# Two transformer blocks on one core: a fifth plain product block in each FFN, and five smaller edits around it

## The chip, the cores and the metric

The kernel runs on one core of a Trainium2 chip. The metric is the time of one execution on the device, in microseconds (us). Engines are named as in the profile: PE is TensorE (matmuls), DVE is VectorE, ACT is ScalarE, POOL is GpSimd, SP is the queue that issues the transfers of the weights.

## What is computed

Two transformer blocks follow each other, with 512 positions, a width of 1024 and float32 values. The first block has a mixer of two attentions and one FFN; the second an FFN, a mixer of sparse attention and retention, another FFN and a last norm. The three FFNs have the same form, and most of the change lies in them:

```python
def _swiglu(x, w_gate, w_up, w_down):
    return (jax.nn.silu(x @ w_gate) * (x @ w_up)) @ w_down

h = h + swiglu(rms_norm(h, norm_ffn_g), w_ffn_gate, w_ffn_up, w_ffn_down)      # f0, in the first block
...
h = h + 0.5 * _swiglu(_rmsnorm(h, ...), ...)                                   # f1 and f2, in the second
```

The hidden width is 2816. In the second mixer, the keys and values of the sparse attention are compressed by small networks (`gelu(blk @ w1) @ w2`), whose weights w1 come into the text below. The norm of the second mixer's input has gains of its own.

## The kernel before, in words

**Precision.** Each float32 operand is held as a high and a low part, and each product is three matmuls: high by high, high by low, low by high. The high part of a weight is a cast on ACT (`wh`, L235 and L300), the low part a subtraction on DVE (`wl`, L236 and L303) or, for some, on POOL. The operand x has `xh` (an ACT cast, L363) and `xl` (a DVE subtraction, L370).

**An FFN** (`ffn`, L1324). The 2816 hidden columns are 22 blocks of 128, in two halves of 11. After each half the down product of that half is added to the residual `xs`. In the first half the first `NPLAIN` blocks, here 4, are plain products: g and u each take 8 x 3 matmuls of 128x512, into one bank each of the two "mm" banks. All other blocks are units (`unit`, L1225): a product scheme that needs seven quarter products in place of eight, each 12 matmuls of 128x256, in the order B11, T1, T4 of the unit before, T2, B21, B22, T3. T4 of a unit is held back (`pending`) and run by `flush()` in the next unit, or behind the last one. A unit's weight sums (s13, s24) are made by DVE in PSUM tiles with the tag "ss", two tiles of two banks each.

**The entry of an FFN.** The first plain block is computed on x without its norm, since the norm's factor is not known yet. It is summed over the columns and spread to all partitions by two matmuls with a diagonal matrix (`spread`, L440, `diag` by DVE L437), and ACT copies the result to `rb` (L442). Each plain block then takes, in this order, fg = g x rb (DVE L1356), tanh (ACT L1357), fu = u x rb (DVE L1358), u x fg (POOL L1359), ft (DVE L1360), and the high and low parts hh and hl of the result. Behind each of the four blocks `prepare_t` makes a quarter of the operand for the units' T products, th and tl, out of the normed rows y (L1204) and their differences ts; `prepare_b`, behind the last plain block, rewrites xh and xl as the parts of y, for the units' B products. The unit's first product, B11, reads these xh and xl; its result is copied by ACT into tile "fu" (L1251), the same tile that holds u of the plain blocks (one buffer), and T2 is added in the same bank after that copy.

**What sets the order.** A scheduler orders each engine's instructions from the program's text and its own estimates. `in_order` pins the units of a first half in the order of the text, and in a second half only the units from number NPLAIN on, so the first NPLAIN units of a second half are left to the scheduler. Weights come by the SP queue, two blocks ahead.

**The second mixer** (`second_mixer`, L1401). It computes keys, values and gates by tokens (L584 to L586) on x without its norm; ACT scales the result by the norm's factor into `kvg` (L1408). Among these products the norm's factor is spread as in an FFN. `renorm` then multiplies xs by gain and rb (DVE L469) and casts xh (ACT) and xl (DVE) anew for the products that follow. The weights w1 of the compression come by POOL's own transfers (L1601), two tiles at a time, with a cast on ACT and a subtraction on POOL (L370); their products are L1607 and L1608.

**The end** (`last`, L1961). The second down product of f2 is computed by tokens, two groups t of 256 rows, with L1982 for its products and with the transposed residual (`turn_out`, L1954) in between. The result is added to the residual (L2009), squared and summed, normed and stored. It begins with a flush of the last unit's T4 and a new set of PSUM banks:

```python
self.flush()()
self.psum("ps4")
```

Of the kernel before, what the change touches and what calls it, by code (L numbers as in the profile page):

```python
# [10 lines left out]
F32 = mybir.dt.float32  # L11
# [8 lines left out]
P = 128  # L20
# [9 lines left out]
RAW_BUFS, PART_BUFS, AHEAD = 4, 5, 2  # L30
NPLAIN = 4
KEEP = 2
# [301 lines left out]
class Build:  # L334
# [989 lines left out]
    def ffn(self, tag, scale, gain, hooks, on_out, begun=None, each=None, last=None):  # L1324
        nc, att = self.nc, self.att
        n = 0
        self.th, self.tl, self.ynorm = [], [], {}
        for half in range(2):
            hh, hl = [], []
            for i in range(11):  # L1330
                if half or i >= NPLAIN:
                    if i in (0, NPLAIN):
                        start = len(self.traced())
                    self.unit(f"{tag}{half}{i}", hh, hl, i)
                    if i == 10:
                        self.in_order(start)
                    continue
                acc = []
                for w in "gu":
                    wh, wl = self.ws.next(f"{tag}{w}{half}{i}")  # L1340
                    self.ws.run_ahead()
                    b = self.bank("mm")
                    self.drain(self.tgroup(b, [(wh[:, k, :], wl[:, k, :], self.xh[k], self.xl[k]) for k in range(KD)]))
                    acc.append(b)
                    if n < len(hooks):
                        hooks[n]()
                    n += 1
                    if n == 2 * NPLAIN - 1:
                        u = self.first_unit(f"{tag}0{NPLAIN}")
                        u.hi24()  # L1350
                        u.lo24()
                if i == 0 and begun is not None:
                    begun()
                tl = lambda t, bufs=1: att.tile([P, 512], F32, tag=t, name=self.nm(t), bufs=bufs)
                g, th, u = tl("fg"), tl("ft", 2), tl("fu")
                nc.vector.tensor_tensor(out=g, in0=acc[0], in1=self.rb, op=ALU.mult)  # L1356
# [4 lines left out]
                self.put_hidden(i, th, 0.5, hh, hl)  # L1361
                self.prepare_t(i, gain)
                if i == NPLAIN - 1:
                    self.prepare_b()
            if half == 1 and last is not None:
                last(hh, hl)
                return
            for m in range(KD):
# [14 lines left out]
                if half == 0 and each is not None:  # L1383
                    each(half, m)
                if scale == 1.0:
# [7 lines left out]
    def second_mixer(self, acc, qpool, eq):  # L1393
# [21 lines left out]
        for m in range(KD):  # L1415
            self.renorm(m, self.xs[m], self.gain("mix_norm_2", m))

        turned = [0]
# [154 lines left out]
    def nsa_keys(self, kvg, need, N):  # L1573
# [17 lines left out]
        for kind in "kv":  # L1591
# [7 lines left out]
            for q in range(4):  # L1599
                w1 = kp.tile([P, 4, 256], F32, tag="w1", name=self.nm("w1"), bufs=2)  # L1600
                nc.gpsimd.dma_start(out=w1, in_=w1v[:, 4 * q:4 * q + 4, :])  # L1601
                wh, wl = (kp.tile([P, 4, 256], F32R, tag=f"w1{a}", name=self.nm("w1"), bufs=2) for a in "hl")
                self.hi(wh, w1)
                self.lo(wl, w1, wh, eng=nc.gpsimd)
# [259 lines left out]
    def main(self):  # L1864
# [53 lines left out]
        def each(half, m):  # L1918
            x = self.xs[m]
            nc.vector.scalar_tensor_tensor(out=x, in0=x, scalar=gf(m), in1=N["rbf"], op0=ALU.mult, op1=ALU.mult)  # L1920
# [40 lines left out]
        def last(hh, hl):  # L1961

            self.flush()()
            self.psum("ps4")
            mm = nc.tensor.matmul
# [3 lines left out]
            for t in range(2):  # L1969

                cut = [((0, 256), (256, 512)) if (t, i, f) == (1, 1, 1) else ((0, 512),) for i in range(2) for f in range(2)]
                tags = self.TOKTAGS[t] + ("mm",)
                acc = [[self.bank(tags[q + n]) for n in range(len(c))] for q, c in enumerate(cut)]
                held = []
# [10 lines left out]
                for k in range(11):  # L1985
# [5 lines left out]
                    for q in range(4):  # L1991
                        for n in range(len(cut[q])):
                            products(w, k, q, n)
                    if t == 0 and k == 0:
                        nc.gpsimd.dma_start(out=gb, in_=I["final_norm_2"][None, :].to_broadcast([P, D]))
                    if t == 0:
# [48 lines left out]
```

## Time and profile before

| | us |
|---|---|
| median of three runs | 2081.18 |
| lowest and highest | 2079.14, 2083.57 |
| the profiled execution | 2081.28 |
| its span, first to last instruction | 2079.4 |
| PE busy in it | 2021.3 (97%) |
| DVE busy | 1479.1 (71%) |
| ACT busy | 1047.5 (50%) |
| POOL busy | 557.3 (27%) |

The profiled execution takes 1.9 us more than its span, for what lies around the first and the last instruction. PE is busy nearly everywhere, so its waits are few and can be counted one by one. The busy shares of the other engines say little: they are means over a long program, and an engine with a share of 71% can be the last to finish in one stretch. In the views below, a bracket behind a row is the time that the engine stood idle before it, and what ended that.

### The profile page before, as it was taken

To read this page: it belongs to the slowest core of one execution; us is meant where nothing else is said; L and a number is where in the kernel's file an instruction comes from. 1 tells how busy PE (TensorE), PEld (TensorE's weight loads), DVE (VectorE), ACT (ScalarE), POOL (GpSimd) and SP (SyncE) were. 2 spreads that over 40 slices of the span, in tenths; PEclk is the share of its full clock that TensorE was granted. 3 is DMA by queue.
4 is the path that set the end of the run, shared out by engine and by line. 5 is a ranking of instruction groups with operands and counts; after the bars stand their busy time and mean duration, and the time that the engine had idled before them with its cause. 6 is when DMAs were issued, how large, how long until landed. Compare 5 with 4: busy or idle time off the path is not lost. (4 is left out here: it accounts for less than half of the span.)

```text
span 2079.4 us, 31555 instructions
## 1 busy us (share of the span) xinstructions
PE 2021.3 (97%) x11802; PEld 1750.8 (84%) x11802; DVE 1479.1 (71%) x2745; ACT 1047.5 (50%) x1959; POOL 557.3 (27%) x469
## 2 busy tenths in 40 slices
PE   9999999999999999999998999999999999999998
PEld 7787878789899879899986778888888887989987
DVE  7678775776587588568648799888457658746865
ACT  7666753354355435345434576666343333534554
POOL 2233232331132334123234211110412232412310
PEclk9999999999999999999999999999999999999999
DMA  7323254123234313333465322222633441333343
GB/s 204 78 73 84 92 169 130 63 79 113 93 107 121 117 51 97 107 101 106 123 169 141 94 61 78 77 70 68 184 118 105 134 139 51 100 112 99 105 158 128
DMA packets 229528, 223.62 MB, mean 108 GB/s; under 512 B 16784, under 2 KB 190992, under 8 KB 229376
## 3 DMA queue, kind: packets, MB, share of 16 engines
q1 hardware_dynamic: 222992, 203.94, 32.6%
q0 software_dynamic: 5024, 15.90, 2.5%
q8 instruction: 93, 1.52, 0.3%
q10 hardware_dynamic: 1360, 1.77, 0.3%
q14 instruction: 59, 0.48, 0.1%
HBM read 204.11 MB, written 14.68 MB: 105 GB/s over the span
## 5 line engine op out<-in xcount | busy, mean ns | idle before, releaser
L236 DVE TENSOR_TENSOR wl<-raw,wh 128x1024 fp32r<-128x1024 f32 (+5 forms) x261 | 311.2, 1195 | 165.9 <-ACT wh L235 164.5
L235 ACT CAST wh<-raw 128x1024 fp32r<-128x1024 f32 (+5 forms) x261 | 245.9, 945 | 358.1 <-PE mm L397 285.5
L396 PE MATMUL mm<-xh,wh 128*128 128x512 f32 x888 | 364.7, 411 | 11.5 <-ACT kvg L1408 5.1
L397 PE MATMUL mm<-xl,wh 128*128 128x512 f32 x888 | 351.6, 396 | 0.6 <-DVE xl L370 0.5
L398 PE MATMUL mm<-xh,wl 128*128 128x512 f32 x888 | 351.4, 396 | 0.0
L303 POOL TENSOR_TENSOR wl<-raw,wh 128x512 fp32r<-128x512 f32 x108 | 140.9, 1325 | 292.5 <-PE mm L1195 177.1
L396 PEld LDWEIGHTS mm<-xh,wh 128*128 128x128 f32 x888 | 168.5, 190 | 40.9 <-DVE fg L1356 5.9
L398 PEld LDWEIGHTS mm<-xh,wl 128*128 128x128 f32 x888 | 167.6, 189 | 35.7
L397 PEld LDWEIGHTS mm<-xl,wh 128*128 128x128 f32 x888 | 168.6, 190 | 26.9 <-DVE xl L370 2.1
L398 PE MATMUL mm<-hh,wl 128*128 128x512 f32 x440 | 173.4, 394 | 0.0
L397 PE MATMUL mm<-hl,wh 128*128 128x512 f32 x440 | 172.5, 392 | 0.0
L396 PE MATMUL mm<-hh,wh 128*128 128x512 f32 x440 | 170.8, 388 | 0.0
L1195 PE MATMUL mm<-th,wh 128*128 128x256 f32 x432 | 121.1, 280 | 12.2 <-ACT fu L1251 12.2
L303 POOL TENSOR_TENSOR wld<-raw,whd 128x512 fp32r<-128x512 f32 x54 | 74.8, 1386 | 213.1 <-DVE s13f L284 129.1
L613 ACT ACTIVATE P<-s,st 128x128 f32<-128x128 f32 (+1 forms) x192 | 101.4, 529 | 58.4 <-DVE st L608 54.3
L1195 PE MATMUL mm<-th,wl 128*128 128x256 f32 x432 | 120.7, 279 | 0.0
L1195 PE MATMUL mm<-tl,wh 128*128 128x256 f32 x432 | 120.7, 279 | 0.0
L1195 PE MATMUL pt<-xh,wh 128*128 128x256 f32 x432 | 120.2, 278 | 0.0
L1195 PE MATMUL pt<-xl,wh 128*128 128x256 f32 x432 | 120.0, 278 | 0.0
L1195 PE MATMUL pt<-xh,wl 128*128 128x256 f32 x432 | 119.8, 277 | 0.0
L363 ACT CAST ph<-pt 128x128 fp32r<-128x128 f32 x192 | 80.3, 424 | 54.4 <-PE pt L631 53.3
L451 POOL TENSOR_TENSOR sacc<-sacc,sq 128x512 f32<-128x512 f32 x36 | 57.2, 1589 | 165.3 <-ACT sq L449 162.6
(481 smaller groups left out, 5490.1 us busy)
## 6 DMA issues: line engine op xcount, KB each, us to landing
raw<-in_gu_f SPq DMA_DIRECT2D x132, 512.0 KB
raw<-in_w_in SPq DMA_DIRECT2D x79, 512.0 KB
raw<-in_ffn_w_down SPq DMA_DIRECT2D x22, 512.0 KB
raw<-in_ffn_w_down SPq DMA_DIRECT2D x24, 384.0 KB
sp_th<-gt SPq DMA_DIRECT2D x32, 256.0 KB
raw<-in_w_out SPq DMA_DIRECT2D x16, 512.0 KB
raw<-in_ffn_w_down SPq DMA_DIRECT2D x24, 320.0 KB
raw<-in_w_ffn_down SPq DMA_DIRECT2D x16, 384.0 KB
```

The costliest lines, as they stand in the source:

```text
L235: nc.scalar.copy(p[0][:, :nk * nc_], src)
L236: nc.vector.tensor_tensor(out=p[1][:, :nk * nc_], in0=src, in1=p[0][:, :nk * nc_].bitcast(F32), op=ALU.subtract)
L303: (eng or self.ws.b.nc.vector).tensor_tensor(out=p[1], in0=src, in1=p[0].bitcast(F32), op=ALU.subtract)
L363: self.nc.scalar.copy(out, in_)
L396: mm(acc, lhsT=lh, rhs=rh, start=start, stop=False)
L397: mm(acc, lhsT=lh, rhs=rl, start=False, stop=False)
L398: mm(acc, lhsT=ll, rhs=rh, start=False, stop=stop)
L451: (eng or nc.gpsimd).tensor_tensor(out=acc, in0=acc, in1=dst, op=ALU.add)
L613: nc.scalar.activation(p, b, AF.Exp, bias=st[:, 0:1], scale=-1.0, accum_out=st[:, 1:2])
L1195: self.nc.tensor.matmul(acc, lhsT=l[:, sl], rhs=r, start=start and k + n == 0, stop=k == 3 and n == 2, skip_group_check=True)
```

## The change

1. `NPLAIN` goes from 4 to 5: each first half has five plain blocks and six units instead of four and seven. In each second half five units instead of four are left to the scheduler.
2. u of a plain block has a tile of its own ("sq" of the small pool) in place of the units' "fu".
3. Block 1 accumulates g and u in one "ss" tile of two banks (`early`) instead of the two "mm" banks.
4. `prepare_b` stands ahead of the last plain block's elementwise work in the text, and `prepare_t` is called for the first four blocks alone.
5. The residual's scaling that f1 issues in its first down product (`each`) is ordered behind the last DVE instruction of the first half's units.
6. The ACT casts of w1 in the second mixer are ordered behind the last cast of `renorm`.
7. `last` no longer begins with the flush and the new banks. The first group's accumulators are two "ss" tiles, the second group's the "mm" and "pt" banks and half of a third "ss" tile; the flush, with T4 of the last unit, follows the first 12 products.

```diff
@@ -28,7 +28,7 @@
 NEG = -1e30
 MAGIC = 12582912.0
 RAW_BUFS, PART_BUFS, AHEAD = 4, 5, 2
-NPLAIN = 4
+NPLAIN = 5
 KEEP = 2
 
 
@@ -1334,12 +1334,19 @@
                     self.unit(f"{tag}{half}{i}", hh, hl, i)
                     if i == 10:
                         self.in_order(start)
+                        self.last_step = [x for x in self.traced() if x.engine == mybir.EngineType.DVE][-1]
                     continue
                 acc = []
                 for w in "gu":
                     wh, wl = self.ws.next(f"{tag}{w}{half}{i}")
                     self.ws.run_ahead()
-                    b = self.bank("mm")
+                    if i == 1:
+
+                        if w == "g":
+                            early = self.ps.tile([P, 1024], F32, tag="ss", name=self.nm("early"), bufs=2)
+                        b = early[:, 512 * (w == "u"):512 * (w == "u") + 512]
+                    else:
+                        b = self.bank("mm")
                     self.drain(self.tgroup(b, [(wh[:, k, :], wl[:, k, :], self.xh[k], self.xl[k]) for k in range(KD)]))
                     acc.append(b)
                     if n < len(hooks):
@@ -1351,17 +1358,18 @@
                         u.lo24()
                 if i == 0 and begun is not None:
                     begun()
+                if i == NPLAIN - 1:
+                    self.prepare_b()
                 tl = lambda t, bufs=1: att.tile([P, 512], F32, tag=t, name=self.nm(t), bufs=bufs)
-                g, th, u = tl("fg"), tl("ft", 2), tl("fu")
+                g, th, u = tl("fg"), tl("ft", 2), self.small.tile([P, 512], F32, tag="sq", name=self.nm("u"), bufs=1)
                 nc.vector.tensor_tensor(out=g, in0=acc[0], in1=self.rb, op=ALU.mult)
                 nc.scalar.activation(th, g, AF.Tanh, scale=0.5)
                 nc.vector.tensor_tensor(out=u, in0=acc[1], in1=self.rb, op=ALU.mult)
                 nc.gpsimd.tensor_tensor(out=u, in0=u, in1=g, op=ALU.mult)
                 nc.vector.scalar_tensor_tensor(out=th, in0=th, scalar=1.0, in1=u, op0=ALU.add, op1=ALU.mult)
                 self.put_hidden(i, th, 0.5, hh, hl)
-                self.prepare_t(i, gain)
-                if i == NPLAIN - 1:
-                    self.prepare_b()
+                if i < 4:
+                    self.prepare_t(i, gain)
             if half == 1 and last is not None:
                 last(hh, hl)
                 return
@@ -1381,7 +1389,8 @@
                         u.lo24()
                 x = self.xs[m]
                 if half == 0 and each is not None:
-                    each(half, m)
+                    with self.tc.issue_after(self.last_step):
+                        each(half, m)
                 if scale == 1.0:
                     nc.vector.tensor_tensor(out=x, in0=b, in1=x, op=ALU.add)
                 else:
@@ -1414,6 +1423,7 @@
                 self.rb = self.spread(self.r_tok, "rb")
         for m in range(KD):
             self.renorm(m, self.xs[m], self.gain("mix_norm_2", m))
+        self.normed = [x for x in self.traced() if x.engine == mybir.EngineType.Activation][-1]
 
         turned = [0]
 
@@ -1600,7 +1610,8 @@
                 w1 = kp.tile([P, 4, 256], F32, tag="w1", name=self.nm("w1"), bufs=2)
                 nc.gpsimd.dma_start(out=w1, in_=w1v[:, 4 * q:4 * q + 4, :])
                 wh, wl = (kp.tile([P, 4, 256], F32R, tag=f"w1{a}", name=self.nm("w1"), bufs=2) for a in "hl")
-                self.hi(wh, w1)
+                with self.tc.issue_after(self.normed):
+                    self.hi(wh, w1)
                 self.lo(wl, w1, wh, eng=nc.gpsimd)
                 for j in range(4):
                     k = 4 * q + j
@@ -1960,8 +1971,6 @@
 
         def last(hh, hl):
 
-            self.flush()()
-            self.psum("ps4")
             mm = nc.tensor.matmul
             ov = self.out[0].rearrange("(t p) d -> t p d", p=P)
             turned = turn_out()
@@ -1969,8 +1978,12 @@
             for t in range(2):
 
                 cut = [((0, 256), (256, 512)) if (t, i, f) == (1, 1, 1) else ((0, 512),) for i in range(2) for f in range(2)]
-                tags = self.TOKTAGS[t] + ("mm",)
-                acc = [[self.bank(tags[q + n]) for n in range(len(c))] for q, c in enumerate(cut)]
+                two = lambda: self.ps.tile([P, 1024], F32, tag="ss", name=self.nm("two"), bufs=2)
+                if t == 0:
+                    acc = [[b[:, f * 512:(f + 1) * 512]] for b in (two(), two()) for f in range(2)]
+                else:
+                    acc = [[self.bank(a)] for a in ("mm", "mm", "pt", "pt")]
+                    acc[3].append(two()[:, 0:512])
                 held = []
 
                 def products(w, k, q, n):
@@ -1992,6 +2005,7 @@
                         for n in range(len(cut[q])):
                             products(w, k, q, n)
                     if t == 0 and k == 0:
+                        self.flush()()
                         nc.gpsimd.dma_start(out=gb, in_=I["final_norm_2"][None, :].to_broadcast([P, D]))
                     if t == 0:
                         next(turned, None)
```

On PE in f1, at the end of the first plain block: the last matmul of block 0, the four spread matmuls (two broadcasts, `pt`), and block 1. Before:

```order
L398 MATMUL mm_7562<-xh_7103,wl_7472 128x512
L440 MATMUL pt_7587<-diag_7592,ones_r 128x512 x2
L440 MATMUL pt_7599<-diag_7604,ones_r 128x512 x2
L396 MATMUL mm_7644<-xh_7096,wh_7502 128x512
L397 MATMUL mm_7644<-xl_7104,wh_7502 128x512
L398 MATMUL mm_7644<-xh_7096,wl_7503 128x512
```

The same place now:

```order
L398 MATMUL mm_7504<-xh_7045,wl_7414 128x512
L440 MATMUL pt_7529<-diag_7534,ones_r 128x512 x2
L396 MATMUL early_7586<-xh_7038,wh_7444 128x512
L397 MATMUL early_7586<-xl_7046,wh_7444 128x512
L398 MATMUL early_7586<-xh_7038,wl_7445 128x512
L396 MATMUL early_7586<-xh_7039,wh_7444 128x512
L440 MATMUL pt_7541<-diag_7546,ones_r 128x512
L397 MATMUL early_7586<-xl_7047,wh_7444 128x512
L398 MATMUL early_7586<-xh_7039,wl_7445 128x512
L440 MATMUL pt_7541<-diag_7546,ones_r 128x512
```

Block 1 goes to the tile `early`, and the second broadcast stands among its matmuls instead of ahead of them.

On ACT at the first unit of f0: xh are prepare_b's casts, hh the last plain block's result, fu the unit's copy of B11 (L1251). Before:

```order
L363 CAST xh_3638<-y_4108 128x512
L363 CAST xh_3639<-y_4197 128x512
L363 CAST xh_3640<-y_4295 128x512
L365 ACTIVATE hh_4289<-ft_4282 128x512
L1251 COPY fu_4326<-mm_4324 128x256
L1256 COPY ff_4327<-pt_4325 128x256
```

Now:

```order
L363 CAST xh_3638<-y_4107 128x512
L363 CAST xh_3639<-y_4196 128x512
L363 CAST xh_3640<-y_4285 128x512
L1251 COPY fu_4399<-mm_4397 128x256
L365 ACTIVATE hh_4393<-ft_4386 128x512
L1256 COPY ff_4400<-pt_4398 128x256
```

The copy now stands ahead of hh, which needs the last plain block's ft, and directly behind the xh casts.

On ACT at the start of the second mixer: w are the casts of w1, rb the copy of the spread factor, wh weight casts, xh the casts of renorm, kvg the scaled keys and values. Before:

```order
L235 CAST wh_11298<-raw_11131 128x1024
L363 CAST w_1153_11388<-w_1152_11386 128x1024
L363 CAST w_1156_11420<-w_1155_11418 128x1024
L442 COPY rb_11227<-s_11217 128x512
L235 CAST wh_11329<-raw_11161 128x1024
L363 CAST xh_10710<-xs_3584 128x512
L363 CAST xh_10711<-xs_3585 128x512
L1408 ACTIVATE kvg<-mm_11123,rs_11185 128x304
L1408 ACTIVATE kvg<-mm_11124,rs_11185 128x304
```

Now, with the place to which the w1 casts have gone:

```order
L235 CAST wh_11122<-raw_10965 128x1024
L235 CAST wh_11182<-raw_11015 128x1024
L442 COPY rb_11111<-s_11101 128x512
L235 CAST wh_11213<-raw_11045 128x1024
L363 CAST xh_10594<-xs_3584 128x512
L363 CAST xh_10595<-xs_3585 128x512
L363 CAST xh_10596<-xs_3586 128x512
L1417 ACTIVATE kvg<-mm_11007,rs_11069 128x304
...
L363 CAST xh_10600<-xs_3590 128x512
L363 CAST xh_10601<-xs_3591 128x512
L363 CAST w_1147_11272<-w_1146_11270 128x1024
L363 CAST w_1150_11304<-w_1149_11302 128x1024
```

The two casts of w1 have moved from ahead of rb to behind the last xh; one more xh stands ahead of kvg.

## Rows read from the trace of the kernel before

**Rows 1.** PE's waits: line, what it waited for, us in total, times, longest.

```profile
PE mm L1195 <- ACT fu L1251: 12.2, 3, 4.5
PE mm L396 <- ACT kvg L1408: 5.1, 1, 5.1
PE mm L396 <- DVE fg L1356: 4.6, 2, 2.3
...
PE mm L1195 <- DVE xl L370: 3.2, 6, 0.8
PE mm L1195 <- DVE fw L1285: 2.5, 2, 2.0
...
PE mm L396 <- DVE fu L1358: 1.6, 2, 1.0
...
PE pt L440 <- DVE diag L437: 1.2, 1, 1.2
```

**Rows 2.** Windows: span, busy us (count) by engine, granted clock, DMA share, GB/s.

```profile
388.00:391.00 3.00, 2.92 (x7) 2.34 (x8) 1.83 (x4) 0.63 (x1) 2.30 (x2) 0.50 0.51 175
1727.40:1731.00 3.60, 3.60 (x16) 2.93 (x17) 2.41 (x4) 0.57 (x2) 2.43 (x2) 1.00 0.43 150
2005.80:2009.00 3.20, 3.20 (x10) 2.52 (x10) 2.59 (x5) 0.63 (x1) 0.00 (x0) 0.50 0.82 268
```

**Rows 3.** Timeline of PE in a plain block: start us, duration, instruction, [idle before].

```profile
395.80 0.39 PE L396 MATMUL mm<-xh,wh 128*128 128x512 f32 x1
...
397.17 0.39 PE L396 MATMUL mm<-xh,wh 128*128 128x512 f32 x1
```

**Rows 4.** Timeline of PE, the first matmul of f0's block 1.

```profile
388.08 0.79 PE L396 MATMUL mm<-xh,wh 128*128 128x512 f32 x1 [2.29 <-DVE fg L1356]
```

**Rows 5.** Timelines of DVE, then of all engines, at f0's first unit.

```profile
423.42 1.09 DVE L370 TENSOR_TENSOR xl<-y,xh 128x256 fp32r<-128x256 f32 x3
...
427.16 0.68 DVE L1358 TENSOR_TENSOR fu<-mm,rb 128x512 f32<-128x512 f32 x1
...
429.60 0.69 DVE L1360 SCALAR_TENSOR_TENSOR ft<-ft,fu 128x512 f32<-128x512 f32 x1 [1.16 <-POOL fu L1359]
...
430.86 0.35 ACT L1251 COPY fu<-mm 128x256 f32<-128x256 f32 x1
```

**Rows 6.** Groups of DVE, 387.3 to 423.5: count | busy us, mean ns | idle before.

```profile
L1356 DVE TENSOR_TENSOR fg<-mm,rb 128x512 f32<-128x512 f32 x4 | 2.7, 679 | 0.0
L1360 DVE SCALAR_TENSOR_TENSOR ft<-ft,fu 128x512 f32<-128x512 f32 x3 | 2.6, 859 | 1.5 <-POOL fu L1359 1.5
L236 DVE TENSOR_TENSOR wl<-raw,wh 128x1024 fp32r<-128x1024 f32 x2 | 2.4, 1222 | 2.4 <-ACT wh L235 2.4
```

**Rows 7.** Line L370 in f0 (ns, min/median/max), and POOL's timeline there.

```profile
L370 DVE TENSOR_TENSOR tl<-ts,th x8: 674/679/1780, 395.8 to 422.8; 128x512 fp32r<-128x512 f32 x8
...
402.46 1.67 POOL L1359 TENSOR_TENSOR fu<-fu,fg 128x512 f32<-128x512 f32 x1 [2.90 <-DVE fu L1358]
```

**Rows 8.** Timelines of ACT, DVE and POOL at the second mixer's start.

```profile
1091.40 1.05 ACT L363 CAST w<-w 128x1024 fp32r<-128x1024 f32 x1 [1.18 <-DMA w<-in_cmp_k_w]
1092.36 0.57 ACT L442 COPY rb<-s 128x512 f32<-128x512 f32 x1
...
1092.96 4.42 DVE L469 SCALAR_TENSOR_TENSOR xs<-xs,gains,rb 128x512 f32<-128x512 f32 x3 [4.28 <-ACT rb L442]
...
1093.81 2.35 POOL L370 TENSOR_TENSOR w<-w,w 128x1024 fp32r<-128x1024 f32 x1
...
1097.28 1.32 ACT L1408 ACTIVATE kvg<-mm,rs 128x304 f32<-128x304 f32 x3
```

**Rows 9.** Line L1601, the transfers of w1 by POOL: issue to landing.

```profile
DMA to landing us min/median/max: 4.1/4.4/5.5
```

**Rows 10.** Timeline of PE at the end of f2's last unit: T3's last, T4's first.

```profile
2002.03 0.28 PE L1195 MATMUL mm<-th,wl 128*128 128x256 f32 x1
2004.35 0.36 PE L1195 MATMUL mm<-th,whd 128*128 128x256 f32 x1 [2.04 <-DVE fw L1285]
```

## The prediction

> **What bounds the kernel now.** I read the list of TensorE's waits first [rows 1]. It is the right place to start because matmuls fill nearly the whole span, so that a change can win only where TensorE stands still, where its clock is low, or where matmuls go away. Each row names what TensorE waited for, the total, the number of waits and the longest. Six of the seven rows lie in four places that the edits touch. Three are the entries of the three FFNs (f0 near 380 us, f1 near 735, f2 near 1720): from the end of the first plain block to the first units. There stand the wait for the first product's elementwise work (fg L1356, two of 2.3 us), for a bank (fu L1358), for the norm's broadcast (diag, f1 alone), for the low parts of the rewritten operand (xl L370, six) and, largest, for the first unit's copy into "fu" (L1251, three of about 4 us). The fourth place is the start of the second mixer, one wait of 5.1 us for kvg. A last one is the final unit's T4, 2.0 of the fw row.
>
> Then I read the granted clock by windows [rows 2]. After the waits at 388.08 and 2004.35 the clock stands at 0.50, the 1.2 GHz level, for some 3 us; after f2's equally long wait, just ahead of 1727.4, it stays at 1.00, so the fall does not follow the length of a wait alone. In 3.0 us at half clock TensorE does 1.5 us of work, so such a stretch costs **1.5 us** on top of its wait. There are six, of which the rows show the first and the last: two in f0, one in f1, one in f2 (behind the copy), one in the mixer, one at the end.
>
> A wait also costs a little more than its row says: from the last matmul of T3 to the first of T4 it is 2.32 us from start to start where the pace would be 0.11, so 2.21 lost, and the list says 2.04 [rows 10]. I add 0.2 us for each wait.
>
> **Why the entries wait.** At the first unit [rows 5] the copy must wait until "fu" is free, since it is both u of the last plain block and e of the unit. VectorE comes to that u only at 427.16, behind the xl's; GpSimd multiplies it; VectorE reads it at 429.60; the copy starts at 430.86 and T2 at 431.27. VectorE reached the first xl at 423.42 because it had worked without a break worth the name since 387.3: it is the busy engine of the entry, and TensorE catches up with it at the end.
>
> **One more plain block instead of a unit (three times).** A plain block is 48 matmuls of 512 columns, a unit 84 of 256: 24,576 against 21,504 columns. Six steps of 512 columns take 1.37 us [rows 3], 0.446 ns a column, so each exchange adds 1.37 us to TensorE; I take 1.4, **4.2 us** for three. On the other side it gives VectorE a block of 48 x 0.228 = 10.96 us more before the xl's are due, for a small addition to its list: one more each of fg, u, ft and hl (u and hl have fg's shape: 0.68, 0.68, 0.86, 0.68), two more splits wl (1.22 each) and one sum of fg's shape (0.68) [rows 6]: 6.0 us, less seven overlaps of some 0.08, so 5.5.
>
> **u apart, "early" in the sum banks.** With u in its own buffer the copy's chain through GpSimd and ft is gone altogether. With "early", block 1 no longer needs the banks that block 0's fg and u free, so it starts where the wait of 2.29 us [rows 4] began, at 385.8. Four blocks then end at 385.8 + 43.8 = 429.6. VectorE starts its list at the same time as before (the norm's broadcast sets that) and needs 423.42 - 387.3 = 36.1, plus 5.5: 428.9. So its first xl starts 0.7 us ahead of TensorE instead of being late. In f1, where the row of the diag wait shows 1.2 us, the second broadcast now stands among block 1's matmuls, and they hide most of it.
>
> What is late next: the last block's tanh needs fg, which VectorE reaches just before the first xl, and ScalarE then casts seven more xh ahead of the copy, whose start I put at 0.2 to 0.5 us behind T2's due time; the banks of blocks 3 and 4 can each be up to 0.9 us late, as the fu L1358 row is now. I leave **1.0 us** of waits in each entry; the ends are 0 and the 2.5 of one wait as it is now.
>
> Sum of the entries: the rows fg 4.6, fu 1.6, xl 3.2, copy 12.2 and diag 1.2 make 22.8 [rows 1]; fourteen waits at 0.2 add 2.8; four half-clock stretches add 6.0: 31.6. Off go 3.0 that stays and 4.2 of longer products: **24.4 us** saved. Prepare_b ahead of the last block's elementwise work is part of this and has no price of its own.
>
> **The casts behind the renorm.** In the mixer the rb copy stands on ScalarE behind two casts of compression weights, the second of which waited for its transfer until 1091.40; VectorE then idled 4.28 us for rb, and kvg came at 1097.28 [rows 8]. With the casts moved behind the last renorm cast, rb comes when its matmuls are done, and VectorE's 4.28 us go; GpSimd's split, beside which three xs took 4.42 us, moves away too. One renorm cast more now stands ahead of kvg. I take kvg 4.4 us earlier, and leave 0.7 to 1.7, middle 1.2, of the wait. Price: GpSimd issues the third compression weight only when it has split the first, which now comes after the renorm, and a transfer takes 4.4 us to land [rows 9], a cast 1.05 and a split 2.35. Nothing in this trace shows how late that is against its matmuls; between nothing and one wait of 2.5 I take 1.2. Saved: 5.1 + 0.2 + 1.5 - 1.2 - 1.2 = **4.4 us**.
>
> **The end.** The twelve matmuls of the first down product, 12 x 0.228 = 2.7 us, now run between T3 and T4, in banks that the last units do not use, and cover the 2.0 that T4 waits for fw. Saved: 2.0 + 0.2 + 1.5 = **3.7 us**.
>
> **The residual scaling** moves from between the units' VectorE work to behind it. The list is the same; hl of the last unit can come one instruction of fg's size, 0.7 us, later behind it in f1, and in each second half five units instead of four are left to the scheduler. I take 0.5 us off, between 0 and 1.5.
>
> Together 24.4 + 4.4 + 3.7 - 0.5 = 32.0. The profiled execution took 2081.28 us, its span 2079.4, and the median of the three runs is 2081.18, so the forecast is **2049 us**.
>
> **A rule that speaks against it.** Of eight tl's of one shape in f0's entry the median took 0.68 us and one 1.78, and that one ran beside GpSimd's product of u and g (1.67 us, from 402.46) [rows 7]. The Trainium skill ("SBUF — State Buffer", section "Who interferes with whom") says that a VectorE instruction with two SBUF inputs and a GpSimd instruction that reads SBUF share a port pair, held for a whole instruction while the other fully blocks; the trace agrees, with 1.1 us beside one of four such products. By that rule the fifth product can block VectorE once more in each FFN.
>
> **Rivals.** (S) One blocked operation more in each entry, 1.1 us each, is more than the 0.7 us of cover, and the blocked operations that are there land beside xl's: each entry keeps 1.1 more, 3.3 in all: 2052. For it speaks the 1.78 us row, against it that only one of eight was hit.
>
> (B) VectorE stays the bound of the entries: bank waits and ScalarE's queue eat the 0.7 us, each entry keeps one wait of 2.5 and its half-clock stretch of 1.5, 4.0 instead of 1.0: 2049 + 9 = 2058. It decides once VectorE's list grows by some 8 us instead of 5.5. For it: its list is the tight one in all three entries. Against: two idle groups in it, 2.4 and 1.5 us [rows 6], can take in some delay.
>
> (C) The late compression weight makes a wait of 2.5 with a clock fall: 2.8 more, 2052.
>
> (D) The waits go but the low clock stays, since waits of equal length had it and had it not [rows 2]: six stretches, 9 us, 2058.
>
> (E) Slower. If VectorE sets the pace of the whole entry and not only its end, its 5.5 us more lengthen each entry in full, 16.5 us, while the waits and stretches there stay; less the mixer's and the end's 8.1, that is 2081 + 8.4 = 2090. It decides from about 11 us of new VectorE delay in each entry, for which no row speaks.
>
> (N) The new order does not hold what the edits say, for example because the scheduler's free units give back what is won, and the time is within 0.2%: 2081.
>
> **How the numbers follow.** Forecast 0.58, S 0.13, B 0.14, C 0.05, D 0.05, E 0.03, N 0.02. All residuals at nothing give 2049 - 3.0 - 2.4 - 0.5 = 2043; B and D reach 2058. I put the range at 2041 to 2060, with about 1 in 10 on either side. A measurement of this kernel can tell about 0.2%, 4 us: its runs lie within 2079.14 to 2083.57. Faster 0.95, same 0.02, slower 0.03.
>
> **What will show it.** The rows fg L1356 and copy L1251 should be gone from the list of waits, or under 1 us each; xl under 2 us; kvg under 2; fw down to 0.5. At 0.50 clock none of the six stretches should be left. VectorE's first xl in f0 should start between 428 and 430 us. I am wrong if a new row of several us appears on a bank of blocks 3 or 4 (B), on POOL w at the compression product (C), or if tl's and xl's mean lengths grow (S).

## The result, and the profile after

The changed kernel takes **2061.63 us** (median of four, 2061.42 to 2062.82) against 2080.47 for the kernel before beside it: a ratio of 0.9907, interval 0.9893 to 0.9921. The forecast was 2049, the range 2041 to 2060. The direction was right, but of the 32 us only 18.8 came, and the time lies 1.6 us above the range.

The trace shows where most of the rest is. TensorE's waits in the changed kernel, in the columns of [rows 1] (line, what it waited for, us in total, times, longest):

```profile
PE pt L1195 <- ACT ff L1256: 7.2, 3, 2.4
...
PE mm L397 <- DVE xl L370: 1.9, 3, 1.4
...
PE s L1618 <- DVE blkhl L370: 2.4, 1, 2.4
...
PE mm L396 <- ACT th L363: 1.4, 3, 0.6
...
PE mm L397 <- DVE hl L372: 0.8, 1, 0.8
...
PE mm L396 <- DVE u L1367: 0.3, 1, 0.3
```

Of the rows in [rows 1], fg L1356, kvg, fw and the copy fu L1251 are gone, as forecast. At the top stands a row that was not there: three waits of 2.4 us on **ff L1256**, the unit's second copy, one in each entry. The granted clock behind each of them (windows as in [rows 2]; the clock is the third number from the right):

```profile
439.90:443.30 3.40, 3.40 (x18) 3.40 (x18) 1.28 (x2) 2.29 (x4) 3.40 (x3) 0.51 0.02 5
788.10:791.50 3.40, 3.40 (x18) 3.40 (x18) 1.27 (x2) 2.28 (x4) 3.40 (x3) 0.50 0.06 10
1768.00:1771.00 3.00, 3.00 (x16) 3.00 (x15) 1.23 (x1) 2.92 (x5) 2.46 (x2) 0.50 0.00 0
```

About 0.5, the 1.2 GHz level, for some 3.4 us each time. Of the six low stretches three are left, then, each behind the new wait.

To compare stages I take the starts of the same PE instructions in the traces: each FFN's broadcast, the last matmul of its first half's units, the first of its second half's, the mixer's broadcast, the end. The last column belongs to the experiment hh_behind, below.

| stage, us | before | after | forecast change | measured change | hh_behind |
|---|---|---|---|---|---|
| start to f0's broadcast | 385.2 | 386.4 | 0 | +1.2 | 385.9 |
| f0's entry and first units | 116.9 | 112.0 | -8.1 | -4.8 | 107.7 |
| f1's entry and first units | 117.3 | 112.6 | -8.1 | -4.7 | 108.4 |
| f2's entry and first units | 116.4 | 111.7 | -8.1 | -4.7 | 107.5 |
| f1's first down product | 56.4 | 57.7 | +0.5 | +1.3 | 57.8 |
| second mixer, broadcast to f2's | 637.4 | 634.9 | -4.4 | -2.5 | 635.5 |
| f2's second half to the end | 182.2 | 177.6 | -3.7 | -4.6 | 177.6 |
| all others | 467.7 | 468.1 | 0 | +0.4 | 468.1 |
| span | 2079.4 | 2061.0 | -32.0 | -18.4 | 2048.7 |

(The forecast's 24.4 for the entries is split in three.) The first row is not the change's doing: in the fourteen profiled executions of this study it lies between 384.3 and 390.1. This is why the experiments are read by their stages as well as by their times.

By the table the span misses its forecast by 13.6 us: 10.2 in the entries, 1.9 in the mixer, 1.2 at the start, 0.8 in f1's down product and 0.4 in the others, less 0.9 won at the end. The greater part is in the entries. One entry in the trace (f0; timelines of DVE, POOL, ACT and PE):

```profile
430.48 0.41 DVE L370 TENSOR_TENSOR xl<-y,xh 128x256 fp32r<-128x256 f32 x1
...
434.57 0.68 DVE L1367 TENSOR_TENSOR u<-mm,rb 128x512 f32<-128x512 f32 x1
...
437.01 0.69 DVE L1369 SCALAR_TENSOR_TENSOR ft<-ft,u 128x512 f32<-128x512 f32 x1 [1.17 <-POOL u L1368]
...
435.39 1.59 POOL L1368 TENSOR_TENSOR u<-u,fg 128x512 f32<-128x512 f32 x1 [8.14 <-DVE u L1367]
...
434.19 0.36 ACT L1251 COPY fu<-mm 128x256 f32<-128x256 f32 x1
437.74 0.63 ACT L365 ACTIVATE hh<-ft 128x512 fp32r<-128x512 f32 x1 [3.19 <-DVE ft L1369]
438.27 0.35 ACT L1256 COPY ff<-pt 128x256 f32<-128x256 f32 x1
...
436.01 0.28 PE L1195 MATMUL mm<-th,wl 128*128 128x256 f32 x1
438.68 0.39 PE L1195 MATMUL pt<-xh,wh 128*128 128x256 f32 x1 [2.40 <-ACT ff L1256]
```

VectorE reaches the first xl at 430.48, where I had put it at 428.9 plus this run's 1.2 us of later start; PE does not wait for it. Then follows the old chain, unbroken: u (434.57, behind seven xl), GpSimd's product (435.39), ft (437.01), hh (437.74). The first copy, fu, is now ahead of hh and goes at 434.19 without a wait. But ff stands *behind* hh on ScalarE, starts at 438.27, and PE's next product, B21, follows it at 438.68 after 2.40 us.

### The profile page after: what moved, and what is told of

The parts are those of the page before. It is cut to its first block, busy times and chain, and to the rows that moved or that the text cites. A ratio compares the mean times of both kernels' runs of the same rounds, so it can differ in the third digit from the quotient of the medians.

```text
span 2061.0 us, 31305 instructions
## 1 busy us (share of the span) xinstructions
PE 2019.5 (98%) x11694; PEld 1746.3 (85%) x11694; DVE 1466.9 (71%) x2727; ACT 1040.6 (50%) x1944; POOL 550.1 (27%) x463
## 5 line engine op out<-in xcount | busy, mean ns | idle before, releaser
L236 DVE TENSOR_TENSOR wl<-raw,wh 128x1024 fp32r<-128x1024 f32 (+5 forms) x267 | 321.4, 1206 | 164.8 <-ACT wh L235 163.7
L235 ACT CAST wh<-raw 128x1024 fp32r<-128x1024 f32 (+5 forms) x267 | 252.2, 948 | 359.5 <-PE mm L397 289.5
L303 POOL TENSOR_TENSOR wl<-raw,wh 128x512 fp32r<-128x512 f32 x102 | 133.4, 1329 | 267.1 <-PE mm L1195 152.0
L303 POOL TENSOR_TENSOR wld<-raw,whd 128x512 fp32r<-128x512 f32 x51 | 69.5, 1362 | 217.6 <-ACT whd L300 130.3
L1195 PE MATMUL pt<-xh,wh 128*128 128x256 f32 x408 | 114.9, 282 | 7.2 <-ACT ff L1256 7.2
L1195 PE MATMUL pt<-xl,wh 128*128 128x256 f32 x408 | 114.8, 281 | 0.0
L1195 PE MATMUL pt<-xh,wl 128*128 128x256 f32 x408 | 114.8, 281 | 0.0
L1195 PE MATMUL mm<-th,wh 128*128 128x256 f32 x408 | 113.3, 278 | 0.0
L1195 PE MATMUL mm<-tl,wh 128*128 128x256 f32 x408 | 112.9, 277 | 0.0
L1195 PE MATMUL mm<-th,wl 128*128 128x256 f32 x408 | 112.8, 276 | 0.0
```

Of the source, the lines that this page charges most:

```text
L235: nc.scalar.copy(p[0][:, :nk * nc_], src)
L236: nc.vector.tensor_tensor(out=p[1][:, :nk * nc_], in0=src, in1=p[0][:, :nk * nc_].bitcast(F32), op=ALU.subtract)
L303: (eng or self.ws.b.nc.vector).tensor_tensor(out=p[1], in0=src, in1=p[0].bitcast(F32), op=ALU.subtract)
L1195: self.nc.tensor.matmul(acc, lhsT=l[:, sl], rhs=r, start=start and k + n == 0, stop=k == 3 and n == 2, skip_group_check=True)
```

## Experiments

All differ from the changed kernel by the few lines shown; all_three and the kernels below whose names begin with hh_ start from hh_behind instead (hh_behind itself from the changed kernel). The theory H: the chain u, GpSimd, ft, hh was not removed but moved by one place in ScalarE's queue. The rival R: ScalarE or VectorE as a whole sets the pace of the first unit, and ff is only the last to come.

### hh_behind: hh taken out from between the two copies

```diff
-                self.put_hidden(i, th, 0.5, hh, hl)
+                if i == NPLAIN - 1:
+                    self.held = lambda th=th, i=i: self.put_hidden(i, th, 0.5, hh, hl)
+                else:
+                    self.put_hidden(i, th, 0.5, hh, hl)
...
         nc.scalar.copy(e[:, 256:512], r1)
+        if self.held is not None:
+            self.held()
+            self.held = None
```

> The changed kernel, and one thing more: hh and hl of the last plain block are issued behind the first unit's second copy (L1267) instead of between its copies fu and ff. Theory H (the chain of GpSimd's product and ft was not removed, it moved one place down ScalarE's queue: hh waits for ft, ff waits behind hh, B21 waits for ff): the three waits on ff (2.4 us each, 2.56 by starts) and the low clock behind them (1.6 us each) go, 12.5 us less than the changed kernel's 2061.6, with up to 1.5 us given back elsewhere: 2049 to 2051. Rival R (ScalarE or VectorE as a whole sets the first unit's pace, and the name ff is only who came last): a wait of about 2 us stays under another name in each entry, 2059 to 2062.

Measured: **2049.66 us** (0.9847 of the kernel before, 0.9832 to 0.9862), 12 us under the changed kernel and the fastest kernel of this study. The row ff is gone from its waits, and nothing took its place. ScalarE at f0's first unit:

```profile
433.94 0.36 ACT L1251 COPY fu<-mm 128x256 f32<-128x256 f32 x1
434.50 0.37 ACT L1256 COPY ff<-pt 128x256 f32<-128x256 f32 x1 [0.20 <-PE pt L1195]
...
436.63 0.38 ACT L1267 COPY fu<-mm 128x256 f32<-128x256 f32 x1
438.61 0.64 ACT L365 ACTIVATE hh<-ft 128x512 fp32r<-128x512 f32 x1 [1.60 <-DVE ft L1373]
```

The copies go at 433.94, 434.50 and 436.63; hh waits 1.60 us for ft at 438.61, and nobody waits for hh. H holds, R falls. The stage table's last column gives 4.2 to 4.3 us for each entry, which is the wait (2.56 from start to start) and its low clock (the other 1.6 to 1.8).

### slow_chain: the chain made longer

```diff
+                if i == NPLAIN - 1:
+                    d = self.small.tile([P, 2, 512], F32, tag="diag", name=self.nm("again"), bufs=1)
+                    nc.gpsimd.tensor_tensor(out=d[:, 0, :], in0=u, in1=g, op=ALU.mult)
```

(with the real product issued behind it, and ff behind hh)

> The changed kernel with the suspected chain made longer: ahead of the last plain block's product u x g GpSimd makes the same product once more, into a scratch tile that nothing reads (some 1.5 us, three times); ff is held behind hh, so that ScalarE's order stays that of the changed kernel. Theory H: GpSimd's product is on the chain to B21, so each wait on ff grows by the product's length, 1.3 to 1.6 us: 4 to 5 us more, 2065.5 to 2066.5. Rival R (the chain only happens to come last, ScalarE or VectorE sets the pace): 2061 to 2062.5.

Measured: 2068.65 us (0.9943, 0.9928 to 0.9958), 7.0 more and 2.2 above H's interval. The row of PE's waits, and GpSimd in f0:

```profile
PE pt L1195 <- ACT ff L1258: 11.3, 3, 3.8
...
435.37 1.61 POOL L1376 TENSOR_TENSOR again<-u,fg 128x512 f32<-128x512 f32 x1 [8.15 <-DVE u L1373]
437.06 1.26 POOL L1378 TENSOR_TENSOR u<-u,fg 128x512 f32<-128x512 f32 x1
```

The wait on ff grew from 7.2 to 11.3, 1.4 us for each added product of 1.26 to 1.61: GpSimd is on the path. What goes beyond 4.1 us is 1.7 in the entries, where the low clock lasts longer in f0 and f2 (these entries are 1.9 and 2.6 us longer, f1's 1.3), and 1.5 us in the mixer, where this edit does nothing: there the clock falls behind the wait on blkhl this time.

### u_first: the chain shortened at its start

```diff
-                    self.prepare_b()
+                    self.prepare_b(range(4))
...
                 nc.vector.tensor_tensor(out=u, in0=acc[1], in1=self.rb, op=ALU.mult)
+                if i == NPLAIN - 1:
+                    with self.tc.issue_after(self.traced()[-1]):
+                        self.prepare_b(range(4, KD))
```

> The changed kernel with the chain shortened at its start: prepare_b's second four blocks (xh, xl 4 to 7) are issued behind the last plain block's u, so VectorE comes to u after three xl instead of six; the scheduler then also puts hh behind ff and one weight cast. Theory H: the three waits on ff and their low clock go, as in hh_behind: 2049 to 2051. Rival R: xl 4 to 7 come later and B21 waits for them instead: 2058 to 2062.

Measured: 2055.41 us (0.9885, 0.9868 to 0.9901), between the two. The row ff is gone, but a third name has come (PE's wait, then ScalarE in f0):

```profile
PE mm L1195 <- ACT fu L1267: 3.9, 3, 1.3
...
433.46 0.37 ACT L1256 COPY ff<-pt 128x256 f32<-128x256 f32 x1 [0.20 <-PE pt L1195]
...
437.27 0.63 ACT L365 ACTIVATE hh<-ft 128x512 fp32r<-128x512 f32 x1 [2.49 <-DVE ft L1372]
437.81 0.99 ACT L300 CAST wh<-s13f 128x1024 fp32r<-128x1024 f32 x1
438.70 0.38 ACT L1267 COPY fu<-mm 128x256 f32<-128x256 f32 x1
```

hh, still waiting for ft, now holds a weight cast and behind it the copy L1267, three waits of 1.3 us, without low clock. The number of H (2049 to 2051) was missed for H's own reason: I had looked at ff alone and not at what is queued behind hh in its new place. (u comes after four xl here instead of seven; the numbers of what was expected count one less in both.)

### u_in_fu: u back in the units' tile

```diff
-                g, th, u = tl("fg"), tl("ft", 2), self.small.tile([P, 512], F32, tag="sq", name=self.nm("u"), bufs=1)
+                g, th, u = tl("fg"), tl("ft", 2), tl("fu")
```

> The changed kernel with u of the plain blocks back in the units' tile fu. hh then stands ahead of the first copy, so T2 instead of B21 waits for the chain, 1.4 us earlier in PE's order. Theory H (a tile of its own moves the wait by one quarter product and no more): 1.2 to 1.6 us more in each entry, 2065 to 2067. Rival (the tile is what matters, as the prediction had it): the full 4.1 us of each entry back, 2070 or more.

Measured: 2067.59 us (0.9936, 0.9921 to 0.9951), 6.0 more, 0.6 above H's interval; the entries are 1.3 to 1.8 us longer. The wait is again that of the kernel before:

```profile
PE mm L1195 <- ACT fu L1251: 11.8, 3, 4.0
```

11.8 against the 12.2 of [rows 1]. So the separate tile alone moved the wait from the first copy to the second and won about 1.6 us an entry, while I had priced it at the whole wait.

### no_early and hh_no_early: block 1 in the mm banks again

```diff
-                    if i == 1:
+                    if False:
```

> The changed kernel with block 1 again in the two mm banks. Theory H: the waits for fg (2.3 us in f0 and f2) and one low clock (1.5) come back, but VectorE's list, which ends the entry, is not moved by them, so the later wait on ff shrinks by as much: 0 to 3 us more, 2061 to 2065. Rival, the prediction's reading (each wait has its own price): 2 x 2.5 + 1.5 + bank waits of 1.6 = 8 us more, 2069 to 2070.

> The kernel hh_behind (hh of the last plain block behind the first unit's copies), with block 1 back in the two mm banks. Theory M (masking: in the changed kernel the chain behind VectorE ended the entry, so a wait at block 1 was repaid at ff; with the chain out of the way nothing repays it): the waits for fg, 2.3 us in f0 and f2, f1's broadcast 1.8 and some low clock of 1.5 count in full: 5 to 8 us over hh_behind's 2049.7, 2055 to 2058. Rival (the sum banks for block 1 are worth nothing in any surroundings): 2049 to 2051.

Measured: no_early 2059.35 us (0.9893, 0.9876 to 0.9909), 2.3 **less** than the changed kernel, where H allowed 0 to 3 more; hh_no_early 2054.76 us (0.9875, 0.9861 to 0.9890), 5.1 more than hh_behind. In no_early:

```profile
PE mm L396 <- DVE fg L1365: 5.0, 3, 2.3
...
PE pt L1195 <- ACT ff L1256: 2.3, 3, 1.2
```

The waits for fg are back with 5.0, those on ff shrank from 7.2 to 2.3, by 4.9. Together they are as long as before (7.3 against 7.2). None of the low stretches behind ff is left; one stands behind fg in f2 instead; with two such stretches fewer the three entries are 2.9 us shorter together. The chain behind VectorE's list ends at its own time; a wait earlier in the entry only fills what TensorE would have waited later. With hh out of the way nothing pays such a wait back, and the same edit is worth 5 us. This is the masking that theory M says (a wait costs nothing while a longer chain ends the stage), at the lower edge of its 5 to 8 us.

### four_blocks and hh_four: four plain blocks

```diff
-NPLAIN = 5
+NPLAIN = 4
```

(and prepare_b behind the last prepare_t again, as it has to be)

> The changed kernel with four plain blocks instead of five (prepare_b again behind the last block's elementwise work, since the fourth prepare_t comes there), all else as changed. Theory H, with VectorE's list as the bound of the entry: without the fifth block PE reaches the first unit at about 385.8 + 4 x 10.96 - 10.96 = 418.7 and the first xl comes at 423.4, so each entry waits some 4.7 us there, keeps its chain behind it (2.4) and a low clock (1.5), and saves 1.4 of longer products: 3 to 5 us more in each, 2071 to 2077. Rival: the fifth block only costs, the other edits do the work: 4 us less, 2057.

> The kernel hh_behind with four plain blocks instead of five. Theory M: the fifth block covers VectorE's list, and without it the waits for xl come back, in f0 and f2 4.4 us each with their low clock, in f1 2.5; less 2.0 of small waits that go and 4.2 of shorter products that is 4 to 6 us over hh_behind: 2053 to 2056. Rival (the fifth block only costs, as the 2059.8 of four_blocks against 2061.6 seems to say): 1.8 to 4.2 us under hh_behind, 2045 to 2048.

Measured: four_blocks 2059.77 us (0.9896, 0.9881 to 0.9911), 1.9 less than with five blocks; hh_four 2062.31 us (0.9913, 0.9896 to 0.9930), 12.7 more than hh_behind. Both my numbers were wrong, in opposite directions. In four_blocks:

```profile
PE mm L1195 <- DVE xl L370: 5.3, 7, 1.2
...
PE pt L1195 <- ACT ff L1256: 2.3, 2, 1.4
...
PE mm L1195 <- ACT fu L1267: 1.5, 1, 1.5
```

The waits for xl are back with 5.3, but not 4.7 in each entry: the scheduler had put xl's between the last tl's, so that the first came at 420.4 and not at 423.4. In hh_four the first unit's third ScalarE copy is late (a row of PE's waits, then ScalarE and VectorE in f0):

```profile
PE mm L1195 <- ACT fu L1267: 4.9, 2, 3.7
...
431.79 1.01 ACT L300 CAST wh<-s13f 128x1024 fp32r<-128x1024 f32 x1 [5.13 <-DVE s24f L284]
432.69 0.38 ACT L1267 COPY fu<-mm 128x256 f32<-128x256 f32 x1
...
427.58 1.76 DVE L1371 SCALAR_TENSOR_TENSOR ft<-ft,u 128x512 f32<-128x512 f32 x1 [1.20 <-POOL u L1370]
...
431.79 0.70 DVE L284 TENSOR_TENSOR s24f<-s24f,raw 128x512 f32<-128x512 f32 x1
```

The cast of the sums s13 waits 5.13 us for VectorE, whose sums stand behind xl, u and ft; the copy L1267 is queued behind it, and TensorE waits 3.7 us for that copy. This is f0, whose entry is 6.9 us longer than in hh_behind. The entries of f1 and f2 are 3.3 and 3.7 longer; there the waits for xl with their low clock are the greater part (f1 has no wait for L1267, f2 one of 1.2). The fifth block gives VectorE the time for the xl's and for these sums. Its worth is thus -1.9 us in the one surrounding and 12.7 in the other.

### old_casts, old_end, hh_free_scaling, all_three: the smaller edits

```diff
-                with self.tc.issue_after(self.normed):
-                    self.hi(wh, w1)
+                self.hi(wh, w1)
```

> The changed kernel with the casts of w1 left to the scheduler, as before. By the stage's rows: the wait for kvg of 5.1 us and its low clock (1.6) come back, and the changed kernel's waits in that stage (xl 1.6, blkhl 2.5) go: 2 to 4 us more, 2064 to 2066. Rival (the wait only moved along the stage, from kvg to xl and blkhl): within 1 us of 2061.6.

> The changed kernel with the end as before (flush first, then the token banks). The wait of T4 for fw (2.2 by starts) and its low clock (1.5) come back: 3.5 to 4.5 us more, 2065 to 2066. Rival (the end's 4.3 us came from the shorter way to the end and not from the wait): 2061 to 2063.

old_casts took 2064.13 us (0.9919, 0.9905 to 0.9934), old_end, with the flush and the new banks first again, 2066.62 (0.9926, 0.9910 to 0.9943). In old_casts the wait for kvg returns (and blkhl shrinks from 2.4 to 0.2), in old_end the one for fw:

```profile
PE mm L396 <- ACT kvg L1417: 5.5, 1, 5.5
...
PE s L1617 <- DVE blkhl L370: 0.2, 1, 0.2
```

```profile
PE mm L1195 <- DVE fw L1285: 2.0, 1, 2.0
```

The mixer's stage is 3.0 us longer in old_casts, as expected (2 to 4). The end is 5.9 us longer in old_end (183.5 against 177.6), more than the 3.5 to 4.5 expected: the wait costs 2.2 by starts, a second wait of 0.5 on ft L1291 stands behind it, which the changed kernel has not, and the clock is at 0.5 from 1989.4 to 1996.3, in which TensorE is at work for 6.4 us and so loses an estimated 3.2. This makes 5.9, where one low stretch had been expected.

```diff
-                    with self.tc.issue_after(self.last_step):
-                        each(half, m)
+                    each(half, m)
```

> The kernel hh_behind with f1's residual scaling left to the scheduler, as before. Theory S (the scaling behind the units' steps holds hl of the last unit in f1, where the trace has a wait of 0.8 us on hl and the stretch from the first half's last unit to the second half's first is 1.3 us longer than before): 1.0 to 1.4 us less, 2048.3 to 2048.7. Rival (the scaling then stands in the way of the last units' steps, for which it was moved): 0 to 1.5 us more, 2049.7 to 2051.

> The kernel hh_behind, and with it u ahead of the second half of prepare_b (u_first) and f1's scaling free (hh_free_scaling). Theory H: with hh out of the way nothing waits for u any more, so u_first adds nothing: the time of hh_free_scaling, 2048 to 2049. Rival: u's bank (mm) and VectorE's order still cost something in the entries (th 1.5 us in three waits, u 0.3): 2046 to 2047.5.

hh_free_scaling took 2053.51 us (0.9869, 0.9854 to 0.9884), 3.9 **more** than hh_behind, beyond even the rival; all_three 2052.26 us (0.9864, 0.9850 to 0.9879). f1's down product did get back its 1.4 us (56.4 against 57.8), as theory S said, but f1's entry became 4.7 us longer. VectorE's group in that entry, then three of PE's waits:

```profile
L1937 DVE SCALAR_TENSOR_TENSOR xs<-xs,gains,rbf 128x512 f32<-128x512 f32 x6 | 4.5, 748 | 0.0
...
PE mm L1195 <- DVE fw L1288: 1.3, 1, 1.3
...
PE mm L1195 <- DVE xl L370: 1.0, 3, 0.4
PE pt L1195 <- DVE wl L303: 0.9, 1, 0.9
```

Six of the eight scalings, 0.75 us each, fall between 768.2 and 780 into VectorE's list, right where it is late. In the kernel before they were as free, but went only at 782.86 and later, during the wait on the first copy and behind it, and cost nothing; a list that is on time gives them room earlier. The order behind the last step keeps them out of it, and that is what the residual scaling's new place is worth: 3.3 us net by the stages. all_three lies above both of its intervals, since hh_free_scaling, on which they were built, missed its own. It shows 1.3 us less than hh_free_scaling, with times that overlap; in f1, where they differ most by stage, it is 0.75 us. With hh out of the way u_first has little left to do.

## Why the prediction was wrong

**What failed** is one sentence: "With u in its own buffer the copy's chain through GpSimd and ft is gone altogether." The order of ScalarE's instructions at the first unit, which stands among the rows of the change, has hh between the copies fu and ff. I read that the copy had come ahead of hh and did not ask what was now behind it. Three waits on ff of 2.56 us by their starts and three low stretches of 1.6 make 12.5 us, against the 3.0 that I had left for all waits of the entries together. hh_behind takes just this away and lands at 2049.66; slow_chain shows the same chain from the other side. That hh_behind comes within 0.7 us of the forecast is in part luck: against the forecast its entries (2.4) and its end (0.9) are better, and its mixer (2.5), f1's down product (0.9), its start (0.7) and the others (0.4) worse.

**What held, of the entries.** VectorE's list (36.1 us, and 5.5 more) put the first xl within 0.4 us of the forecast time. The waits fg, fu L1358 and diag fell from 4.6, 1.6 and 1.2 to nothing, 0.3 and nothing. In hh_behind the three entries together are 26.8 us shorter than before; the forecast had 24.4. The sum was near, then, for a kernel in which the chain really is gone.

**Rivals.** (B) came near in price, 2058, but not in cause: VectorE was in time, the chain was late. (S) did not happen in the entries: of sixteen tl's and xl's in f0 one tl is long, as before [rows 7]. Other instructions of VectorE's list are longer than the shortest of their kind too, but up to f0's first xl all these excesses sum to some 3.7 us now, against some 4.8 before.

```profile
L370 DVE TENSOR_TENSOR tl<-ts,th x8: 673/679/1786, 397.6 to 421.0; 128x512 fp32r<-128x512 f32 x8
L370 DVE TENSOR_TENSOR xl<-y,xh x8: 415/552/692, 430.5 to 435.2; 128x256 fp32r<-128x256 f32 x4, 128x512 fp32r<-128x512 f32 x4
```

(C) did not happen: the wait for the split of w1 at the compression product is 1.4 us in both kernels (POOL w at L1608 before, L1619 now). (D) did not: the six low stretches of before went with their waits, and the three in the changed kernel follow a wait that is new.

**The mixer** gave 2.5 instead of 4.4 us. kvg is gone from the waits, but xl (1.6 by starts, 1.2 expected of kvg) and blkhl (2.5, for 1.2 of w1) are there. The casts moved GpSimd's splits of w1 to a place where VectorE is needed (ACT, POOL, DVE):

```profile
1081.51 0.59 ACT L442 COPY rb<-s 128x512 f32<-128x512 f32 x1 [2.03 <-PE s L440]
...
1085.28 1.32 ACT L1417 ACTIVATE kvg<-mm,rs 128x304 f32<-128x304 f32 x3
...
1094.99 6.21 POOL L370 TENSOR_TENSOR w<-w,w 128x1024 fp32r<-128x1024 f32 x2
...
1095.50 3.42 DVE L236 TENSOR_TENSOR wl<-raw,wh 128x1024 fp32r<-128x1024 f32 x1
...
1105.61 1.23 DVE L370 TENSOR_TENSOR blkhl<-blkk,blkhl 128x1024 fp32r<-128x1024 f32 x1
```

Two splits took 6.21 us together, where one took 2.35 in [rows 8], and VectorE's wl beside them took 3.42 instead of the 1.22 of [rows 6]. The Trainium skill ("SBUF — State Buffer", section "Who interferes with whom") says that a VectorE instruction with two SBUF inputs contends with a GpSimd instruction that reads SBUF. These rows agree with it. That this delay alone made blkhl late was not tried.

In six of the experiments (four_blocks, u_in_fu, hh_four, hh_no_early, hh_free_scaling, all_three) the wait on blkhl was 0.8 instead of 2.4, though none of their edits touches the mixer. VectorE is not the cause: the splits (6.16 to 6.17) and wl (3.39 to 3.41) are as long there, and the product behind the wait starts 26.6 us after the mixer's broadcast in all of them, as in the changed kernel. TensorE comes to the wait 1.6 us later, since in these six a low stretch begins already 15.6 to 16.0 us after the broadcast, behind the wait on xl. There the low stretch ahead of the wait is paid out of the wait, and behind it the clock stays at 1.00 (1100.5 to 1104.0 in hh_no_early).

**The end** gave 4.6 us for 3.7; in this stage the kernel before had a second wait on fw, 0.5 us at 1937.58 (one of the two in [rows 1]), which is gone too. **The scaling** was mispriced in both directions: hl came 0.8 us late to PE in f1, as said,

```profile
845.40 2.07 DVE L1931 SCALAR_TENSOR_TENSOR xs<-xs,gains,rbf 128x512 f32<-128x512 f32 x3
...
849.78 0.68 DVE L372 SCALAR_TENSOR_TENSOR hl<-ft,hh 128x512 fp32r<-128x512 f32 x1
```

(the scalings, from 845.40 on, stand ahead of hl at 849.78), and the entry of f1 was spared 4.7 us (by hh_free_scaling against hh_behind), which I had not seen at all: I had summed VectorE's list in f0, which has no scalings, and in f1's entry of the kernel before they stood behind the stretch that was summed.

**Start.** 1.2 us of the miss are the part ahead of f0, which varies by itself.

## What to carry to other kernels

An instruction that waits on an in-order queue holds everything behind it. When a wait is taken from one instruction, follow the late operand to where it is now waited for, and read who stands behind that: the same chain had three names here, fu, ff and L1267, one for each place of hh.

An edit has no price of its own while a longer chain ends the stage: the early bank was worth -2.3 us with the chain and 5.1 without, the fifth block -1.9 and 12.7. Break the last chain first, and price the others again after it.

Sum a busy engine's list in every instance of a stage and in the order that the change will give it: f1's entry held scalings that f0's has not, and they move into the list as soon as it has room.

## What the runs showed of the hardware

Whether the clock falls behind a wait is not set by the wait's length. The wait on blkhl in the mixer is 2.36 us in the changed kernel and in hh_behind alike, and in windows just behind it the granted clock stands at 1.00 in the first and 0.51 in the second:

```profile
1107.00:1110.00 3.00, 3.00 (x19) 2.74 (x20) 2.37 (x3) 1.53 (x2) 0.72 (x1) 1.00 0.59 153
```

```profile
1099.10:1102.60 3.50, 3.50 (x13) 3.02 (x12) 1.50 (x3) 1.61 (x2) 2.11 (x1) 0.51 0.58 164
```

By this window the second lost some 1.7 us of work, with the same instructions ahead of the wait. The wait on ff in f0 is 2.4 us in the changed kernel and in old_casts; the low level follows it in the first alone, and f0's entry is 112.0 us in the first and 110.2 in the second. Likewise fg's wait of 2.29 us in f0 was followed by the low level in the kernel before and not in no_early, and in f2 the other way round. Single executions can thus differ by some 1.6 us for each wait of about 2 us that is left, which is a reason of its own to remove such waits; what decides it is open.
